# The first input product of the second layer, with x stationary over one token tile at a time, and four reorderings

## The chip, the cores and the metric

The kernel runs on one core of a Trainium2 chip. The metric is the device time of one execution in microseconds. An execution has an instruction stream for each engine: TensorE (PE in the profile, with its weight loads as PEld), VectorE (DVE), ScalarE (ACT), GpSimd (POOL) and SyncE (SP, which here only starts DMAs).

## The reference

A trunk of two layers works on one sequence of 256 tokens by 2048 features, all in float32. In outline:

```python
# layer 0
z, xbc, dt, q, k, v, gate = split(x @ in0_w)          # 2048 -> 13344 columns
ya = rms_norm(ssd(silu(conv(xbc)), softplus(dt)) * silu(z))
yb = causal_attention(rope(q), rope(k), v) * silu(gate)
x  = layer_norm(alpha * x + concat(ya, yb) @ out0_w)  # 4096 -> 2048
# layer 1
u, gate = split(x @ in1_w)                            # 2048 -> 2 * 2048
y  = gelu(s5(u))                                      # complex diagonal state space scan
ga, gb = split(y @ glu_w)                             # 2048 -> 2 * 2048
x  = layer_norm(alpha * x + (ga * sigmoid(gb) * silu(gate)) @ out1_w)
```

## The kernel before

**Units and their three products.** Every weight matrix is read as units of 512 KB: 256 input rows by 512 columns (`_chunk`), or 512 rows by 256 columns (`_half`). A unit is loaded into a `raw` tile by SP (L233), rounded into a high part `wh` by ACT (L236), and the rest `wl = raw - wh` is made by DVE (L238); `split_to(i)` does this for all units up to `i`. The pool has four buffers each for `raw`, `wh` and `wl`. The activations are kept as a high and a low part too. A product is the sum of high x high, high x low and low x high, on PE, in one of three forms:

- "x" (`xmm`, L282): the activations of one token tile (128 tokens) are the stationary operand, 512 weight columns move: 12 matmuls of 512 columns for a unit. The result has tokens on partitions.
- "w" (`wmm`, L303): 128 weight columns are stationary, 256 tokens move: 24 matmuls of 256 columns for a unit. The result has features on partitions.
- wide (`product_wide`, L336 and L337): weights stationary, the high and low activations move together as 512 columns, then 256 more: 8 pairs for a unit.

**The order of the work.** The instructions are written in program order and placed by a planner (`schedule_with_timeline_sim`), which simulates the engines and fills each engine's stream by priority and readiness. `tc.issue_after(i)` ties instructions to come behind `i` on `i`'s engine. Work other than the products waits in the list `jobs`; `pump` gives out some after each unit. A second list, `back`, is spread evenly over the units up to `goal[0]`; `finish` gives out what is left of it.

**The start.** `product_two` makes B and C together, the first unit of both first. Unit 0 is loaded and split in two pieces of 256 KB (L227 to L229), unit 1 whole. `dt_mm` and the five jobs of `dt_jobs` follow: two with a chain of polynomial steps on POOL (L516 to L527), then `soft4` (from L529), with L533 the DVE step that reads that chain's result, and `turn` (L547), which transposes what comes of it. They stand ahead of the four `cb_job`s.

**Constants of layer 1.** In layer 0's attention stage, `block_jobs(b)` prepares the scan's matrices for 16 blocks: `bars`, `efs`, `fcs` (DVE; `bars` also loads on SP), and for each pair `pes` (PE transposes and small matmuls, L761) and `mts` (six PE matmuls L771, ACT copies and two stores on ACT's queue).

**The seam.** The last output product of layer 0 is `product_apart`: ten units for both token tiles, then the last six (kept in a pool of their own) for tile 0, then the same six for tile 1. When tile 0 is done, `after0` adds the residual (`res0`: L1034, statistics L1035) and normalises (`norm_stats`, `scaled`: L1074 and L1077) while PE works on tile 1. `turned(t, f0, nf)` transposes `nf` blocks of 128 features on PE (`transpose4`, L412), rounds them on ACT (L1086) and makes the low part on DVE (L1090). Blocks 0 to 7 of tile 0 are turned by `mid`, ahead of the last unit of tile 1. Then PE runs 14 matmuls on a zero tile (`warm(WARM1)`, L421), turns two blocks of tile 1, and runs three more (`WARM2`). The first of layer 1's products follows in the form "w", which needs both token tiles of a block of features; the other blocks are normalised and turned by `prelude` between its units. The normalised activations lie in `x1t` with the 256 tokens in the order (token mod 4, token div 4).

**After the seam.** `first1` is the first quarter of u. `u_first` copies it to the tile `ut` (one buffer; L1152), `u_store` writes it to DRAM on POOL's queue (L1147), and the scan's steps (`steps`, two for each of 16 blocks, then `y_load` and `y_split`) go on `back`, with the goal ten units into the gated product. The other u quarters come in the wide form; `total` (L343, L344) adds their two halves. `y_split` (L1274, L1275) makes the high and low parts of y for the gated product, `product_pair`, whose units 6 and 7 are done last; `turn` in `glu_jobs` turns the gated result.

Of the kernel before, what the change touches and what calls it, by code (L numbers as in the profile page):

```python
# [9 lines left out]
F32 = mybir.dt.float32  # L10
F32R = mybir.dt.float32r
AF = mybir.ActivationFunctionType
# [4 lines left out]
P = 128  # L17
# [8 lines left out]
NKEEP = 6  # L26
WARM0 = 8
# [141 lines left out]
def trunk(tc, io, out):  # L169
# [8 lines left out]
    with ExitStack() as top:  # L178
# [34 lines left out]
        keep = [None, range(0)]  # L213

        def split_to(i):
            while nsplit[0] <= min(i, len(units) - 1):
# [5 lines left out]
                if n == 0:  # L222
                    wh = st.tile([P, UK, 512], F32R, tag="wh", name=nm("wh"))
                    wl = st.tile([P, UK, 512], F32R, tag="wl", name=nm("wl"))
                    for k in range(UK):
                        xpart(k)
# [11 lines left out]
                splits[n] = (loaded[-1], high, V.tensor_tensor(wl, raw, wh.bitcast(F32), op=OP.subtract))  # L238
# [38 lines left out]
        def xmm(ps, o, wpair, j, hk, start, stop):  # L277
            (xh, xl, xx), k = hk
            wh, wl = wpair
            sl = slice(o * P, o * P + P)  # L280
            for i, (l, r) in enumerate(((xh, wh), (xh, wl), (xl, wh))):
                T.matmul(ps[o], l[:, k, sl], r[:, j, :], start=start and i == 0, stop=stop and i == 2)  # L282
# [42 lines left out]
        def product_wide(hl, dst, then):  # L325
            for h in range(2):
# [14 lines left out]
                def total(o, ps=ps, h=h):  # L341
                    to = dst()[:, 2 * h + o, :]
                    A.activation(to, ps[o][:, 0:S], AF.Copy)  # L343
                    V.tensor_tensor(to, to, ps[o][:, S : 2 * S], op=OP.add)  # L344
# [22 lines left out]
        def product_two(hl, after):  # L367
            pss = [banks(), banks()]
            order = [(n, u) for u in range(PAIRED) for n in range(2)] + [(n, u) for n in range(2) for u in range(PAIRED, CU)]
            for at, (n, u) in enumerate(order):  # L370
                split_to(at + 3)
                parts = (((0, 1), (0, 1)), ((0, 1), (2,)))
                if at == 0:
# [7 lines left out]
        def product_apart(hl, nu, nk, after, mid=None):  # L381
            ps = banks()
            for u in range(nu - nk):
                split_to(unit[0] + 3 + u)
# [53 lines left out]
        with ExitStack() as l0:  # L438
# [139 lines left out]
            jobs.extend(dt_jobs())  # L578
# [117 lines left out]
            pend = []  # L696

            def block_jobs(b):
# [80 lines left out]
                return [bars, efs, fcs, pes, mts] if b % 2 else [bars, efs, fcs, lambda: pend.append(h)]  # L779
# [6 lines left out]
            def xs_jobs(ps, j):  # L786
# [13 lines left out]
                jobs.extend({0: [cb_job(g) for g in range(4)], 1: [trig_job], 2: [table_job]}.get(j, []))  # L800
# [255 lines left out]
        with ExitStack() as lt:  # L1056
# [22 lines left out]
            def turned(t, f0, nf):  # L1079
# [5 lines left out]
                hv, lv = (x1t[n][:, f0 : f0 + nf, :].rearrange("p f (s c) -> p f s c", s=4)[:, :, :, 32 * t : 32 * t + 32] for n in "hl")  # L1085
# [11 lines left out]
            def after0(ps, t):  # L1097
                def first():
# [4 lines left out]
                    scaled(t, 0, 2 if t else 4, norm_stats(st0, mr0, t))  # L1103

                jobs.append(first)
                jobs.extend([lambda: scaled(1, 2, 2)] if t else [lambda: scaled(0, 4, 4), lambda: scaled(0, 8, 4)])
# [8 lines left out]
            warm(WARM1)  # L1115
            end, tail["v"] = turned(1, 0, 2)
            with tc.issue_after(end.ins):
                warm(WARM2)
            x1 = x1n

            def rest0():
                tail["v"] = turned(1, 2, 2)[1]
# [4 lines left out]
            later = {1: [(1, 1)], 3: [(1, 2)], 5: [(0, 3), (1, 3)]}  # L1127
# [273 lines left out]
```

## Time and profile before

| | |
|---|---|
| median of 3 runs | 1340.22 us (1339.83 to 1340.71) |
| profiled execution, its own time | 1341.48 us |
| its span | 1339.7 us |
| PE busy | 1324.2 us (99%) |
| DVE, ACT, POOL busy | 960.9, 688.7, 336.6 us |
| granted PE clock, mean | 0.996 |
| DMA | 282.74 MB, 211 GB/s |

Times in the profile count from the span's start. L282 is line 282 of the kernel before. Matmuls are pipelined: one row's duration overlaps the next one's, so the rate is read from the starts, or from the chain of waits, where each piece counts only its own share. A busy PE says that instructions are in it, not that they are needed. The seam between the layers lies at about 849 to 886 us.

### The profile page before, as it was taken

The page shows a single profiled execution, that of the slowest core. Times are in us where ns is not written, and L with a number is a line of the kernel's source. Part 1 is how long each engine was busy: PE and PEld are TensorE (multiplying, and loading weights), DVE is VectorE, ACT ScalarE, POOL GpSimd, SP SyncE. Part 2 cuts the span into 40 slices and gives each one's busy share as a digit, 9 for nine tenths or more (in the row PEclk, how much of TensorE's full clock was granted, in tenths as well). Part 3 has the DMA queues.
Part 4 walks back from the last instruction along what each step waited for, and adds up shares of the span by engine and source line. Part 5 has one row for each costly group of instructions (what it writes and reads, how often), then busy time and mean ns, then how long its engine had stood idle before and what let it go on. Part 6 is the DMA issues. An engine that isn't in the chain of part 4 may idle for free.

```text
span 1339.7 us, 21680 instructions
## 1 busy us (share of the span) xinstructions
PE 1324.2 (99%) x8175; PEld 1119.6 (84%) x8175; DVE 960.9 (72%) x1604; ACT 688.7 (51%) x930; POOL 336.6 (25%) x648
## 2 busy tenths in 40 slices
PE   9999999999999999999999999999999999999996
PEld 8988888877888888888888888898888888888885
DVE  5677977876776876778788766749898845555556
ACT  5566668864644554554563444344345644444441
POOL 0042000121036148334887300013343100000001
PEclk9999999999999999999999999999999999999998
DMA  8555555444557557666757768397988675565662
GB/s 309 179 175 183 186 173 173 156 153 158 168 188 232 189 199 237 197 207 202 233 189 245 248 232 310 136 306 237 315 282 303 221 219 187 189 191 188 252 213 83
DMA packets 80729, 282.74 MB, mean 211 GB/s; under 512 B 9840, under 2 KB 12528, under 8 KB 80112
## 3 DMA queue, kind: packets, MB, share of 16 engines
q1 hardware_dynamic: 68112, 239.27, 53.9%
q0 software_dynamic: 7328, 30.42, 6.7%
q10 hardware_dynamic: 5184, 11.67, 2.4%
q8 instruction: 64, 1.05, 0.3%
q14 instruction: 41, 0.34, 0.1%
HBM read 260.34 MB, written 20.97 MB: 210 GB/s over the span
## 4 chain that ended last, share of the span: by engine, by line
PE 94%; POOL 2%; DVE 2%; DMA 1%; issue 1%; ACT 1%; SPq 0%; POOLq 0%; DVEq 0%; ACTq 0%
PE main L282 59%; PE main L336 14%; PE main L337 7%; PE main L303 5%; PE aux L412 2%; PE aux L850 1%; PE aux L761 1%; PE enc L1197 1%; PE dec L1242 1%; PE aux L939 1%; PE aux L971 1%; DVE wl L238 0%; DMA raw<-in_wi 0%; PE dec L1238 0%; POOL ew L527 0%
## 5 line engine op out<-in xcount | busy, mean ns | idle before, releaser
L238 DVE TENSOR_TENSOR wl<-raw,wh 128x1024 fp32r<-128x1024 f32 x431 | 533.0, 1238 | 321.8 <-ACT wh L236 317.6
L236 ACT ACTIVATE wh<-raw 128x1024 fp32r<-128x1024 f32 x431 | 455.7, 1059 | 530.9 <-PE main L282 328.4
L282 PE MATMUL main<-wh,A 128*128 128x512 f32 x1536 | 489.9, 394 | 0.0
L282 PEld LDWEIGHTS main<-wh,A 128*128 128x128 f32 x1536 | 287.8, 188 | 59.1 <-issue 0.3
L282 PE MATMUL main<-wl,A 128*128 128x512 f32 x768 | 300.8, 392 | 0.0
L336 PE MATMUL main<-A,wh 128*128 128x512 f32 x768 | 272.0, 398 | 0.0
L282 PE MATMUL main<-wh,C 128*128 128x512 f32 x768 | 241.4, 392 | 0.0
L337 PE MATMUL main<-A,wl 128*128 128x256 f32 x768 | 215.4, 281 | 0.0
L336 PEld LDWEIGHTS main<-A,wh 128*128 128x128 f32 x768 | 144.2, 188 | 33.9
L282 PEld LDWEIGHTS main<-wh,C 128*128 128x128 f32 x768 | 144.1, 188 | 30.6
L282 PEld LDWEIGHTS main<-wl,A 128*128 128x128 f32 x768 | 144.3, 188 | 29.2 <-issue 0.5
L282 PE MATMUL main<-wl,C 128*128 128x512 f32 x384 | 149.8, 390 | 0.0
L337 PEld LDWEIGHTS main<-A,wl 128*128 128x128 f32 x768 | 144.9, 189 | 0.2
L688 POOL TENSOR_TENSOR c<-c 128x8 f32<-128x8 f32 (+2 forms) x192 | 96.8, 522 | 25.8 <-DMA wb<-c 18.2
L282 PEld LDWEIGHTS main<-wl,C 128*128 128x128 f32 x384 | 72.1, 188 | 14.6
L336 PE MATMUL main<-C,wh 128*128 128x512 f32 x192 | 68.5, 400 | 0.0
L859 POOL TENSOR_TENSOR ssq<-ssq,c 128x256 f32<-128x256 f32 x16 | 18.4, 1147 | 171.6 <-ACT c L857 171.0
L912 POOL TENSOR_TENSOR b<-b 128x128 f32<-128x128 f32 x16 | 10.2, 639 | 194.6 <-DVE b L911 152.1
L337 PE MATMUL main<-C,wl 128*128 128x256 f32 x192 | 53.8, 281 | 0.0
L690 POOL TENSOR_TENSOR c<-c,c 128x4 f32<-128x4 f32 (+2 forms) x96 | 48.0, 500 | 7.4
L303 PE MATMUL main<-A,wh 128*128 128x256 f32 x256 | 44.1, 288 | 1.5 <-ACT wh L236 1.5
L691 POOL TENSOR_TENSOR c<-c,c 128x4 f32<-128x4 f32 (+2 forms) x96 | 45.5, 474 | 0.0
(287 smaller groups left out, 1451.4 us busy)
## 6 DMA issues: line engine op xcount, KB each, us to landing
raw<-in_wi SPq DMA_DIRECT2D x271, 512.0 KB, 3.5
raw<-in_wo SPq DMA_DIRECT2D x96, 512.0 KB, 4.3
raw<-in_wglu SPq DMA_DIRECT2D x64, 512.0 KB, 4.1
wt<-wb POOLq DMA_DIRECT2D x16, 896.0 KB, 8.1
wb<-ob ACTq DMA_DIRECT2D x16, 512.0 KB, 5.3
bc<-in_s5bc SPq DMA_DIRECT2D x16, 256.0 KB, 4.0
wb<-c POOLq DMA_DIRECT2D x16, 256.0 KB, 3.4
wb<-om ACTq DMA_DIRECT2D x16, 128.0 KB, 4.1
```

Source lines behind the costliest of these rows:

```text
L236: high = A.activation(wh, raw, AF.Copy)
L238: splits[n] = (loaded[-1], high, V.tensor_tensor(wl, raw, wh.bitcast(F32), op=OP.subtract))
L282: T.matmul(ps[o], l[:, k, sl], r[:, j, :], start=start and i == 0, stop=stop and i == 2)
L303: T.matmul(pv[o // 2][:, o % 2, :], l[:, j, sl], r[:, k, :], start=first and i == 0 and o % 2 == 0, stop=end and i == 2 and o % 2 == 1, sk ...
L336: T.matmul(ps[o], wh[:, j, sl], xx[:, k, :, :].rearrange("p a n -> p (a n)"), start=first, stop=False, skip_group_check=True)
L337: T.matmul(ps[o][:, S : 2 * S], wl[:, j, sl], xh[:, k, :], start=False, stop=end, skip_group_check=True)
L412: end = T.transpose(dst[:, i * P : i * P + P], s, ident)
L688: G.tensor_tensor(p[:, :, :, 0:m], cs[:, :, :, 1 : m + 1], cs[:, i, :, n : n + 1].unsqueeze(1).to_broadcast([P, 2, 4, m]), op=OP.mult)
L690: G.tensor_tensor(cs[:, 0, :, n + 1 : n + 1 + m], p0[:, 0, :, 0:m], p1[:, 1, :, 0:m], op=OP.subtract)
L691: G.tensor_tensor(cs[:, 1, :, n + 1 : n + 1 + m], p0[:, 1, :, 0:m], p1[:, 0, :, 0:m], op=OP.add)
L761: T.matmul(pk[at : at + 64, 64 * n + a * 16 : 64 * n + a * 16 + 16], d["ev"][:, a, 64 * i : 64 * i + 64], cv[:, a, i, :], start=True, stop ...
L859: G.tensor_tensor(ssq, ssq, jk[:, f, :], op=OP.add)
```

## The change

The first u product is written in the form "x". Its first four units (`NFIRST`) run over token tile 0, the first three of them directly behind the last output product, in place of the filler matmuls; tile 1 is normalised meanwhile on DVE, turned in four steps of four blocks, and the four units run again over tile 1. Units 4 to 7 run over both tiles. The order on DVE is tied from instruction to instruction, the low parts of the weights included (`hold`). The product now has tokens on partitions, so `u_first` copies it out, turns it back with eight transposes two units later, and only then stores it and puts the scan's steps on `back`. The tokens lie in `x1t` as (tile, token mod 4, rest), so that a tile is contiguous; `total`, `y_split` and the gated `turn` put the old order back, some of them in two pieces instead of one.

The four reorderings: unit 1 is loaded and split in two pieces as unit 0 is, and its matmuls are ordered by piece; `soft4` and `turn` of `dt_jobs` come behind the `cb_job`s, a column block later; `mts` of a pair comes behind `bars` of the next block; and `product_apart` prefetches no further than the first four units of the next product.

```diff
...
 NKEEP = 6
+NFIRST = 4
...
         keep = [None, range(0)]
+        hold = [None]
...
                 raw = st.tile([P, UK, 512], F32, tag="raw", name=nm("raw"))
-                if n == 0:
+                if n < 2:
...
                     for k in range(UK):
-                        xpart(k)
+                        if n == 0:
+                            xpart(k)
...
                 wl = pool.tile([P, UK, 512], F32R, tag=tl, name=nm("wl"))
-                splits[n] = (loaded[-1], high, V.tensor_tensor(wl, raw, wh.bitcast(F32), op=OP.subtract))
+                with ExitStack() as pin:
+                    if hold[0] is not None:
+                        pin.enter_context(tc.issue_after(hold[0]))
+                    splits[n] = (loaded[-1], high, V.tensor_tensor(wl, raw, wh.bitcast(F32), op=OP.subtract))
...
             for i, (l, r) in enumerate(((xh, wh), (xh, wl), (xl, wh))):
-                T.matmul(ps[o], l[:, k, sl], r[:, j, :], start=start and i == 0, stop=stop and i == 2)
+                end = T.matmul(ps[o], l[:, k, sl], r[:, j, :], start=start and i == 0, stop=stop and i == 2)
+            return end
...
-        def product_wide(hl, dst, then):
+        def product_wide(hl, dst, then, order=None):
...
                     to = dst()[:, 2 * h + o, :]
-                    A.activation(to, ps[o][:, 0:S], AF.Copy)
-                    V.tensor_tensor(to, to, ps[o][:, S : 2 * S], op=OP.add)
+                    one, two = ps[o][:, 0:S], ps[o][:, S : 2 * S]
+                    if order:
+                        to = to.rearrange("p (s t c) -> p t s c", s=4, t=2)
+                        one, two = (v.rearrange("p (t s c) -> p t s c", s=4, t=2) for v in (one, two))
+                    A.activation(to, one, AF.Copy)
+                    V.tensor_tensor(to, to, two, op=OP.add)
...
                 parts = (((0, 1), (0, 1)), ((0, 1), (2,)))
-                if at == 0:
+                if at < 2:
...
             ps = banks()
+            cap = unit[0] + nu + NFIRST - 1
             for u in range(nu - nk):
-                split_to(unit[0] + 3 + u)
+                split_to(min(unit[0] + 3 + u, cap))
...
             jobs.append(dt_mm)
-            jobs.extend(dt_jobs())
+            dtj = dt_jobs()
+            jobs.extend(dtj[:3])
...
             pend = []
+            late = []
...
-                return [bars, efs, fcs, pes, mts] if b % 2 else [bars, efs, fcs, lambda: pend.append(h)]
+                if b % 2:
+                    late.append(mts)
+                    return [bars, efs, fcs, pes] + ([mts] if b == 15 else [])
+                return [bars] + ([late[-1]] if late else []) + [efs, fcs, lambda: pend.append(h)]
...
                 held.extend([back(0), back(1)])
-                jobs.extend({0: [cb_job(g) for g in range(4)], 1: [trig_job], 2: [table_job]}.get(j, []))
+                jobs.extend({0: [cb_job(g) for g in range(4)] + dtj[3:], 1: [trig_job], 2: [table_job]}.get(j, []))
...
                 pv = px[:, 0 : nf * P].rearrange("p (f c s) -> p f s c", f=nf, s=4)
-                hv, lv = (x1t[n][:, f0 : f0 + nf, :].rearrange("p f (s c) -> p f s c", s=4)[:, :, :, 32 * t : 32 * t + 32] for n in "hl")
+                hv, lv = (x1t[n][:, f0 : f0 + nf, t * P : t * P + P].rearrange("p f (s c) -> p f s c", s=4) for n in "hl")
...
                         res0(tp.tile([P, 2, 512], F32, tag="xr", name=nm("xr")), ps, 3, (t,))
-                    scaled(t, 0, 2 if t else 4, norm_stats(st0, mr0, t))
+                    scaled(t, 0, 4, norm_stats(st0, mr0, t))
...
                 jobs.append(first)
-                jobs.extend([lambda: scaled(1, 2, 2)] if t else [lambda: scaled(0, 4, 4), lambda: scaled(0, 8, 4)])
+                jobs.extend([] if t else [lambda: scaled(0, 4, 4), lambda: scaled(0, 8, 4)])
...
             drain()
-            warm(WARM1)
-            end, tail["v"] = turned(1, 0, 2)
-            with tc.issue_after(end.ins):
-                warm(WARM2)
             x1 = x1n
-
-            def rest0():
-                tail["v"] = turned(1, 2, 2)[1]
...
-            later = {1: [(1, 1)], 3: [(1, 2)], 5: [(0, 3), (1, 3)]}
-            first1 = product("w", x1hl, prelude=lambda u: [turned(0, 8, 4) if u == 3 else None] + [step(t, i) for t, i in later.get(u, [])], first=(((0, 1), (0, 2)), rest0, ((0, 1), (1,))))
+            def first_product():
+                ps = banks()
+                base = unit[0]
+                split_to(base + NFIRST - 1)
+
+                end = {}
+
+                def mm(u, t):
+                    for j in range(UK):
+                        end["i"] = xmm(ps, t, ready[base + u], j, x1hl(u * UK + j), u == 0 and j == 0, u == CU - 1 and j == UK - 1)
+
+                def turn(t, f0):
+                    with tc.issue_after(end["i"].ins):
+                        end["t"], tail["v"] = turned(t, f0, 4)
+
+                def take(u):
+                    hold[0] = tail["v"].ins
+                    split_to(base + u)
+                    hold[0] = None
+                    tail["v"] = splits[base + u][2]
+
+                scaled(1, 4, 4)
+                for u in range(NFIRST - 1):
+                    mm(u, 0)
+                turn(1, 0)
+                with tc.issue_after(end["t"].ins):
+                    mm(NFIRST - 1, 0)
+                scaled(1, 8, 4)
+                turn(1, 4)
+                mm(0, 1)
+                take(4)
+                turn(0, 8)
+                mm(1, 1)
+                turn(1, 8)
+                take(5)
+                mm(2, 1)
+                scaled(0, 12, 4)
+                scaled(1, 12, 4)
+                mm(3, 1)
+                take(6)
+                turn(0, 12)
+                for u in range(NFIRST, CU):
+                    if u == 5:
+                        turn(1, 12)
+                        take(7)
+                    if u > 5:
+                        split_to(base + u + 2)
+                    for t in range(2):
+                        mm(u, t)
+                split_to(base + CU + 2)
+                for u in range(CU):
+                    ready.pop(base + u)
+                unit[0] += CU
+                return ps
+
+            first1 = first_product()
...
             def u_first(ps):
-                ut = u_tile()
-                for i in range(2):
-                    A.activation(ut[:, 2 * i : 2 * i + 2, :].rearrange("p f n -> p (f n)"), ps[i], AF.Copy)
-                u_store(ut, 0)
+                d = {}
+
+                def take():
+                    d["x"] = [w1("p1", [P, 2, 256]).rearrange("p a n -> p (a n)") for t in range(2)]
+                    for t in range(2):
+                        A.activation(d["x"][t], ps[t], AF.Copy)
+
+                def turn():
+                    ut = u_tile()
+                    px = sp.tile([P, 2, 512], F32, tag="enc", name=nm("turn"))
+                    for t in range(2):
+                        transpose4(px[:, t, :], [d["x"][t][:, f * P : f * P + P] for f in range(4)])
+                        A.activation(ut.rearrange("p f (s c) -> p f s c", s=4)[:, :, :, 32 * t : 32 * t + 32],
+                                     px[:, t, :].rearrange("p (f s c) -> p f s c", f=4, s=4), AF.Copy)
+                    u_store(ut, 0)
+                    back.extend([lambda fs=fs: [f() for f in fs] for t, fs in sorted(steps.items())])
+
+                return [take, lambda: None, turn]
...
                 fs = slice(4 * j, 4 * j + 4)
-                A.activation(y5["h"][:, fs, :], yt, AF.Copy)
-                V.tensor_tensor(y5["l"][:, fs, :], yt, y5["h"][:, fs, :].bitcast(F32), op=OP.subtract)
+                for t in range(2):
+                    yv = yt.rearrange("p f (s t c) -> p t f s c", s=4, t=2)[:, t]
+                    hv, lv = (y5[n][:, fs, t * P : t * P + P].rearrange("p f (s c) -> p f s c", s=4) for n in "hl")
+                    A.activation(hv, yv, AF.Copy)
+                    V.tensor_tensor(lv, yv, hv.bitcast(F32), op=OP.subtract)
...
-                    product_wide(x1hl, ut, lambda h, ut=ut, j=j: jobs.append(lambda: u_store(ut(), j)) if h else None)
+                    product_wide(x1hl, ut, lambda h, ut=ut, j=j: jobs.append(lambda: u_store(ut(), j)) if h else None, order=True)
...
                 if j == 0:
-                    jobs.append(lambda ps=ps: u_first(ps))
+                    jobs.extend(u_first(ps))
...
                 if j == 0:
-                    back.extend([lambda fs=fs: [f() for f in fs] for t, fs in sorted(steps.items())])
...
                     transpose4(px, [d["t"][:, o, f * P : f * P + P] for f in range(2) for o in range(2)])
-                    pv = px.rearrange("p (f s c) -> p f s c", f=2, s=4)
-                    ho, lo = (y[:, 2 * j : 2 * j + 2, :].rearrange("p f (c s) -> p f s c", s=4) for y in (y2h, y2l))
-                    A.activation(ho, pv, AF.Copy)
-                    V.tensor_tensor(lo, pv, ho.bitcast(F32), op=OP.subtract)
+                    for f in range(2):
+                        pv = px[:, f * S : f * S + S].rearrange("p (t s c) -> p t s c", t=2, s=4)
+                        ho, lo = (y[:, 2 * j + f, :].rearrange("p (t c s) -> p t s c", t=2, s=4) for y in (y2h, y2l))
+                        A.activation(ho, pv, AF.Copy)
+                        V.tensor_tensor(lo, pv, ho.bitcast(F32), op=OP.subtract)
...
                 jobs.extend([gate, rest, rest, turn])
...
```

## The prediction

> **What bounds the kernel now.** I read the page first, then what TensorE (PE) waited for, then the seam between the two layers in order of time, then the chain.
>
> ```profile
> span 1339.7 us, 21680 instructions
> PE 1324.2 (99%) x8175; PEld 1119.6 (84%) x8175; DVE 960.9 (72%) x1604; ACT 688.7 (51%) x930; POOL 336.6 (25%) x648
> ```
>
> What PE waited for in the whole span (total us, times, longest):
>
> ```profile
> PE main L303 <- ACT wh L236: 1.5, 1, 1.5
> PE main L303 <- DVE C L1090: 1.3, 1, 1.3
> PE aux L421 <- DVE idle L416: 1.0, 1, 1.0
> PE aux L547 <- DVE ew L533: 0.6, 1, 0.6
> ```
>
> PE is busy 99% and waits four times, 4.4 us in all. So nothing can be won by making another engine faster; the time can fall only where PE waits, or where its "busy" time is not needed work. The second kind is found at the seam. PE there, in order of time (start, us, line, count):
>
> ```profile
> 849.57 3.38 PE L421 MATMUL aux<-idle 128*128 128x512 f32 x14
> ...
> 859.71 1.82 PE L412 MATMUL aux<-consts,D 128*128 128x128 f32 x12
> 861.43 0.50 PE L303 MATMUL main<-C,wh 128*128 128x256 f32 x2
> 863.27 0.39 PE L303 MATMUL main<-C,wh 128*128 128x256 f32 x1 [1.34 <-DVE C L1090]
> ...
> 877.01 0.63 PE L336 MATMUL main<-C,wh 128*128 128x512 f32 x2
> ...
> 880.06 0.28 PE L303 MATMUL main<-C,wh 128*128 128x256 f32 x1
> ...
> 885.58 0.40 PE L336 MATMUL main<-C,wh 128*128 128x512 f32 x1
> ```
>
> Three stretches of the seam (us, busy time and count of PE, PEld, DVE, ACT, POOL, then granted clock, DMA share, GB/s):
>
> ```profile
> 849.57:853.70 4.13, 4.13 (x21) 3.17 (x19) 3.92 (x11) 0.59 (x2) 0.00 (x0) 1.00 0.00 0
> ...
> 859.71:863.27 3.56, 2.10 (x16) 1.51 (x14) 3.56 (x6) 2.52 (x4) 0.00 (x0) 1.00 0.47 147
> 863.27:866.69 3.42, 3.42 (x17) 3.42 (x18) 3.13 (x5) 0.00 (x0) 0.00 (x0) 0.54 0.46 158
> ```
>
> From 849.57 to 853.70 PE is fully "busy", but L421 is the filler on the idle tile: real work is two transposes. From 859.71 it turns twelve blocks, does two matmuls and waits for a low part (L1090); then for 3.42 us it works at a granted clock of 0.54. The seam costs time in three ways, and only one of them is a wait.
>
> **The first product.** The rates are in the chain (start, us, work):
>
> ```profile
> 847.48 0.87 PE aux L412 x8
> ...
> 880.23 5.51 PE main L303 x46
> ...
> 1065.06 8.38 PE main L282 x36
> ...
> 1074.30 35.81 PE main L282 x157
> ...
> 1118.96 21.81 PE main L282 x96
> ```
>
> A transpose is 0.87/8 = 0.109 us, a matmul with the weights stationary (L303) 5.51/46 = 0.120. The changed first product is the same 96 matmuls with x stationary as the last row: 8 units x 2 tiles x 6, 21.81 us unbroken. The old one is 192 x 0.120 = 23.0 us.
>
> Before: from 849.57 to 885.58 are 36.01 us. In the 3.05 us from 877.01 to 880.06 PE does eight pairs (L336 and L337), one whole unit of the next product, and only two matmuls of this one (0.24), so 2.81 us come off: 33.2 us.
> After: 21.81 + 24 transposes (8 blocks of tile 0, 16 of tile 1, as before) x 0.109 = 24.4 us, plus the turning back, 8 x 0.109 = 0.9: 25.3 us. The difference is 7.9 us, if PE never waits. Whether it does is decided on DVE, whose order the change pins from end to end:
>
> ```profile
> 848.59 1.29 DVE L1090 TENSOR_TENSOR C<-aux,C 128x512 fp32r<-128x512 f32 x2 [0.62 <-ACT C L1086]
> 849.79 0.68 DVE L1034 SCALAR_TENSOR_TENSOR D<-xr,main 128x512 f32<-128x512 f32 x1
> ...
> 851.60 0.47 DVE L1074 SCALAR_TENSOR_TENSOR D<-D,mr,row 128x256 f32<-128x256 f32 x1
> ...
> 857.61 0.75 DVE L1077 SCALAR_TENSOR_TENSOR D<-D,mr,row 128x512 f32<-128x512 f32 x1
> 858.27 0.75 DVE L1074 SCALAR_TENSOR_TENSOR D<-D,mr,row 128x512 f32<-128x512 f32 x1
> 858.94 1.22 DVE L238 TENSOR_TENSOR wl<-raw,wh 128x1024 fp32r<-128x1024 f32 x1
> 860.07 0.74 DVE L1077 SCALAR_TENSOR_TENSOR D<-D,mr,row 128x512 f32<-128x512 f32 x1
> ...
> 862.53 0.68 DVE L1090 TENSOR_TENSOR C<-aux,C 128x512 fp32r<-128x512 f32 x1
> ```
>
> A normalised piece of 512 (L1074 and L1077) is 1.3 to 1.5 us, a low part of x 0.6 to 0.7, a low part of a weight unit 1.13 to 1.22. Blocks 0 to 7 of tile 0 are finished about 849.9, so units 0 to 3 can run over tile 0 from 849.57, the first three until 853.7. DVE begins tile 1 at 849.79, as before; residual and statistics done, its first piece starts at 851.60 and, at 512 wide and with the reciprocal between, ends about 853.2, just ahead of the first transposes (853.7). I then laid PE's order (six matmuls 1.36, four transposes 0.44) against DVE's chain. The low part of blocks 0 to 3 ends about 855.6, wanted 856.3; low weights of unit 4 at 859.7 and x blocks 8 to 11 at 860.3 and 861.6, wanted 862.2 and 863.6; unit 5 at 862.7, wanted 865; blocks 12 to 15 at 867.4 and 868.0, wanted 868.5; unit 7 at 869.2, wanted 871.2. Every margin is between 0.5 and 2 us: no wait, but little cover. I allow 0.3 us for handovers; the bounds are 0, and 3.5 us if the thin ones all go. Raw weights are not the limit: their four buffers come free with the low parts of units 0 to 3, before the seam, and the prefetch beyond them that the cap removes could not be split anyway, as the split buffers are full.
>
> The clock: 3.42 x 0.46 = 1.6 us of the 7.9 are the stretch at 0.54, which followed 3.56 us of transposes and waiting. [...]
>
> **The turning back** also moves work. The store of the first u block leaves two units (2 x 2.81 = 5.6 us) later, and the scan's steps start with it. POOL's queue carries that store, the loads and the scan's tables behind it. The steps are spread anew over the units left to the same last unit, so the lag is made up on the way; what ends the scan is this:
>
> ```profile
> 1093.05 1.23 DVE L1275 TENSOR_TENSOR A<-ut,A 128x1024 fp32r<-128x1024 f32 x1 [2.58 <-ACT A L1274]
> ```
>
> ```profile
> 1061.32 0.39 PE L282 MATMUL main<-wh,A 128*128 128x512 f32 x1
> ```
>
> The last y is split at 1094.3. The product that needs it starts at 1061.32; 48 of its matmuls come before 1074.30 (a unit of 12, and the 36 at 1065.06), and the 145th reads that y: 1074.30 + 96 x 0.227 = 1096.1. Only 1.8 us of cover. Halving the split (one piece per token tile) adds two fixed costs but lets DVE start sooner; I take 0, with up to 3 us if the last steps fall a unit behind. The single u tile is a further wait: the second u block must wait on ACT until the store has landed, with weight splits queued behind it. The splits run three units ahead of PE (some 8 us), so it costs nothing unless the store takes over twice this:
>
> ```profile
> ud<-ut POOLq DMA_DIRECT2D x2, 512.0 KB, 3.8
> ```
>
> **The start.** PE and ACT at the second unit:
>
> ```profile
> 8.16 0.64 PE L303 MATMUL main<-A,wl 128*128 128x256 f32 x4
> 10.25 2.18 PE L303 MATMUL main<-A,wh 128*128 128x256 f32 x16 [1.46 <-ACT wh L236]
> ```
>
> ```profile
> 6.42 0.63 ACT L228 ACTIVATE wh<-raw 128x512 fp32r<-128x512 f32 x1 [1.43 <-DMA raw<-in_wi]
> 9.14 1.06 ACT L236 ACTIVATE wh<-raw 128x1024 fp32r<-128x1024 f32 x1 [2.09 <-DMA raw<-in_wi]
> 10.11 0.61 ACT L456 ACTIVATE A<-a 128x512 fp32r<-128x512 f32 x1
> 11.09 1.06 ACT L236 ACTIVATE wh<-raw 128x1024 fp32r<-128x1024 f32 x1 [0.37 <-DMA raw<-in_wi]
> ```
>
> In halves, the first half of unit 1 lands about midway between 6.42 and 9.14, say 7.8, and is rounded by 8.4, before PE is done at 8.64. So the 1.6 us gap closes. But unit 2 is rounded at 12.15 whatever is done (ACT waits for its DMA), and PE would want it at 8.64 + 24 x 0.120 = 11.5; it took it at 8.64 + 1.61 + 2.9 = 13.1. Gain 1.0 us, bounds 0 and 1.6. On SP's queue the extra DMA puts the next loads one issue later.
>
> **The other three edits.** The later softplus end (`dtj[3:]`) takes away PE's 0.6 us for L533, which ends POOL's long chain: gain 0.6, bounds 0 and 0.7, as the scan needs it far later. `mts` behind the next block's `bars` moves six matmuls, ACT copies and two stores on ACT's queue past `bars`' load on SP and its DVE work; the list of PE's waits has none there, so 0 from both sides. The permuted layout and split copies in `total`, `y_split` and `turn` cost ACT some 0.2 us a time (2 x 0.63 against 1.06 above) and DVE as little, hidden under PE: 0.
>
> **The sum** for the profiled execution (span 1339.7, its own time 1341.48): 7.9 - 0.3 + 1.0 + 0.6 = 9.2 us less, 1332.3. The median of the runs shown is 1.26 lower than that execution, so 1331.0.
>
> **The rivals.** (1) PE waits at the seam: the planner puts the turning of tile 0's last four blocks ahead of unit 4. These want the normalised piece at 864.2, PE is there at 862.2: 2 us, and what follows inherits up to 1.5 more. For it: the before trace has just such a misplaced turning at 859.71. Against: unit 4 is ready first. 1333 to 1334.5, chance 0.20. [...] Chance 0.06. (3) The change doesn't do what it says: the planner starts no x matmuls at 849.57, and the filler's 3.9 us stay as a wait: 1335. Against: their operands are ready and nothing else is. Chance 0.08. (4) Slower: the scan's tail. Beyond its 1.8 us of cover each us of delay is a us of PE wait; to end over 0.2% slower than before it must lose 9.2 + 2.7 + 1.8 = 13.7 us, five units at the end of the list, then 1343 or more. Against: the same last unit. Chance 0.04.
>
> **How the numbers follow.** The forecast has 0.62; 1331.0 is its own. The upper end 1335.5 takes in rivals 1 and 3; the lower end 1328.8 takes the start at 1.6, no handovers, and a unit's worth (some 1.5 us) for small waits that the records hide. About 0.2% (2.7 us) is what a measurement can tell from no change: all but rival 4 and a mixture of losses to about 1338 clear it. Faster 0.92, same 0.04, slower 0.04.
>
> **What would show it.** Right: no L421 after the first microseconds; x-stationary matmuls directly behind the last output product; clock 1.00 through the seam; the first product ended some 8 to 9 us earlier relative to 849.57; PE's wait list without L533 and with under 0.8 us at unit 2. Wrong: a PE wait on L1090, L1074 or L238 over 1 us in the seam, a second half-clock stretch, or a wait on L1275 at the gated product.

## The result, and the profile after

The changed kernel takes 1338.04 us (median of 22 runs, 1336.15 to 1342.72), the kernel before 1339.97 us in 22 runs beside them (1338.28 to 1343.95). The ratio is 0.9986, with a 95% interval of 0.998 to 0.9992: 1.9 us faster, between 1.1 and 2.7. The forecast was 9.2 us, and its range ended at 1335.5.

The profiled execution after has a time of its own of 1336.96 us. The page:

```profile
span 1335.2 us, 21514 instructions
PE 1318.7 (99%) x8070; PEld 1110.2 (83%) x8070; DVE 960.1 (72%) x1614; ACT 692.6 (52%) x946; POOL 343.4 (26%) x648
```

The two profiled executions are 4.5 us apart, the medians 1.9. The one before lay 1.5 above its median, the one after 1.1 below. So terms read from the two traces add up to more than was won.

What PE waited for after the change (us in total, times, longest):

```profile
PE aux L559 <- DVE ew L545: 2.1, 1, 2.1
PE main L310 <- ACT wh L231: 1.2, 3, 0.5
PE aux L433 <- DVE idle L428: 1.0, 1, 1.0
PE main L343 <- DVE ut L355: 0.7, 1, 0.7
PE main L288 <- ACT C L1103: 0.3, 1, 0.3
```

L545 is L533 of before, L231 and L310 are L228 and L303, L433 is L421, L424 is L412, L343 and L344 are L336 and L337, L288 is L282, L355 is L344, L539 is L527, L559 is L547, L1103 is L1086. The wait on L1090 is gone. The wait on the step behind POOL's chain, which was to go, has grown from 0.6 to 2.1. The wait for the u tile is new.

PE through the seam after the change, in order of time (start, us, line, count):

```profile
848.56 1.03 PE L424 MATMUL aux<-consts,D 128*128 128x128 f32 x8
...
850.81 0.39 PE L288 MATMUL main<-wh,C 128*128 128x512 f32 x1
...
854.90 0.60 PE L424 MATMUL aux<-consts,D 128*128 128x128 f32 x4
...
857.18 0.60 PE L424 MATMUL aux<-consts,D 128*128 128x128 f32 x4
...
858.57 0.60 PE L424 MATMUL aux<-consts,D 128*128 128x128 f32 x4
...
860.86 0.60 PE L424 MATMUL aux<-consts,D 128*128 128x128 f32 x4
...
869.06 1.03 PE L424 MATMUL aux<-consts,D 128*128 128x128 f32 x8
869.85 0.71 PE L343 MATMUL main<-C,wh 128*128 128x512 f32 x2
870.90 0.50 PE L288 MATMUL main<-wh,C 128*128 128x512 f32 x1 [0.34 <-ACT C L1103]
...
876.50 0.40 PE L344 MATMUL main<-C,wl 128*128 128x256 f32 x2
```

The first product reads C from 850.81, directly behind the output product, with no filler between. The next product takes over at 876.50. From these 25.69 us come off the two matmuls of the next product at 869.85 (2 x 0.227), so it takes 25.2 us, one wait of 0.34 included. The same work took 33.2 us before: at the seam 8.0 us were won.

Three stretches after the change (us, busy time of PE, PEld, DVE, ACT, POOL, granted clock, DMA share, GB/s):

```profile
107.20:110.60 3.40, 1.30 (x8) 0.90 (x7) 1.25 (x4) 0.00 (x0) 1.91 (x3) 1.00 0.00 0
110.60:114.00 3.40, 3.40 (x13) 2.61 (x12) 3.34 (x7) 2.06 (x5) 0.00 (x0) 0.50 0.27 60
...
848.50:872.00 23.50, 23.16 (x118) 18.92 (x117) 17.42 (x26) 10.80 (x15) 2.89 (x8) 1.00 0.25 86
```

The clock is full through the seam. The half-clock stretch now stands at 110.6, behind the wait on L545.

To see where time went, the two profiles were laid side by side at equal numbers of columns of the big products done. A unit is 6144 columns, and there are 432. The changed kernel is 0.9 us ahead after the start. Between the 20th and the 30th unit it falls back by 2.6, since the `cb_job`s now come there, and by another 1.5 at the step behind POOL's chain. At the 60th unit, when the same work is done in both, it is 1.1 behind: 2.0 us have been lost. It wins 8.1 at the seam, and gives 2.3 back in the 110 us behind it.

### The profile page after: what moved, and what is told of

The parts are those of the page before. It is cut to its first block, busy times and chain, and to the rows that moved or that the text cites. A ratio compares the mean times of both kernels' runs of the same rounds, so it can differ in the third digit from the quotient of the medians.

```text
span 1335.2 us, 21514 instructions
## 1 busy us (share of the span) xinstructions
PE 1318.7 (99%) x8070; PEld 1110.2 (83%) x8070; DVE 960.1 (72%) x1614; ACT 692.6 (52%) x946; POOL 343.4 (26%) x648
## 4 chain that ended last, share of the span: by engine, by line
PE 95%; POOL 2%; DMA 2%; DVE 1%; ACT 0%; issue 0%; SPq 0%; POOLq 0%; ACTq 0%; DVEq 0%
PE main L288 60%; PE main L343 15%; PE main L344 8%; PE main L310 3%; PE aux L424 2%; DMA raw<-in_wi 1%; PE aux L867 1%; PE aux L775 1%; PE enc L1275 1%; PE dec L1320 1%; PE aux L956 1%; PE aux L988 1%; POOL ew L528 0%; PE dec L1316 0%; DMA ud<-ut 0%; PE aux L785 0%
## 5 line engine op out<-in xcount | busy, mean ns | idle before, releaser
L288 PE MATMUL main<-wh,A 128*128 128x512 f32 x1536 | 489.9, 394 | 0.0
L288 PEld LDWEIGHTS main<-wh,A 128*128 128x128 f32 x1536 | 287.8, 188 | 59.1 <-issue 0.3
L288 PE MATMUL main<-wl,A 128*128 128x512 f32 x768 | 300.7, 392 | 0.0
L343 PE MATMUL main<-A,wh 128*128 128x512 f32 x768 | 272.9, 399 | 0.0
L288 PE MATMUL main<-wh,C 128*128 128x512 f32 x832 | 262.0, 392 | 0.3 <-ACT C L1103 0.3
L344 PE MATMUL main<-A,wl 128*128 128x256 f32 x768 | 215.3, 280 | 0.0
L288 PEld LDWEIGHTS main<-wh,C 128*128 128x128 f32 x832 | 155.6, 188 | 33.5 <-ACT C L1103 1.0
L343 PEld LDWEIGHTS main<-A,wh 128*128 128x128 f32 x768 | 144.8, 188 | 33.5
L288 PEld LDWEIGHTS main<-wl,A 128*128 128x128 f32 x768 | 144.3, 188 | 29.3 <-issue 0.5
L288 PE MATMUL main<-wl,C 128*128 128x512 f32 x416 | 162.3, 390 | 0.0
L344 PEld LDWEIGHTS main<-A,wl 128*128 128x128 f32 x768 | 145.3, 189 | 0.3
L701 POOL TENSOR_TENSOR c<-c 128x8 f32<-128x8 f32 (+2 forms) x192 | 99.8, 538 | 23.6 <-DMA wb<-c 16.0
L288 PEld LDWEIGHTS main<-wl,C 128*128 128x128 f32 x416 | 78.1, 188 | 16.1
L343 PE MATMUL main<-C,wh 128*128 128x512 f32 x192 | 68.4, 400 | 0.7 <-DVE ut L355 0.7
L344 PE MATMUL main<-C,wl 128*128 128x256 f32 x192 | 53.3, 282 | 0.0
L310 PE MATMUL main<-A,wh 128*128 128x256 f32 x256 | 43.5, 284 | 1.2 <-ACT wh L231 1.2
```

The costliest lines, as they stand in the source:

```text
L288: end = T.matmul(ps[o], l[:, k, sl], r[:, j, :], start=start and i == 0, stop=stop and i == 2)
L310: T.matmul(pv[o // 2][:, o % 2, :], l[:, j, sl], r[:, k, :], start=first and i == 0 and o % 2 == 0, stop=end and i == 2 and o % 2 == 1, sk ...
L343: T.matmul(ps[o], wh[:, j, sl], xx[:, k, :, :].rearrange("p a n -> p (a n)"), start=first, stop=False, skip_group_check=True)
L344: T.matmul(ps[o][:, S : 2 * S], wl[:, j, sl], xh[:, k, :], start=False, stop=end, skip_group_check=True)
L701: G.tensor_tensor(p[:, :, :, 0:m], cs[:, :, :, 1 : m + 1], cs[:, i, :, n : n + 1].unsqueeze(1).to_broadcast([P, 2, 4, m]), op=OP.mult)
```

## The experiments

**The softplus end alone.** The kernel before with the `dt_jobs` edit and nothing else:

```diff
-            jobs.extend(dt_jobs())
+            dtj = dt_jobs()
+            jobs.extend(dtj[:3])
...
-                jobs.extend({0: [cb_job(g) for g in range(4)], 1: [trig_job], 2: [table_job]}.get(j, []))
+                jobs.extend({0: [cb_job(g) for g in range(4)] + dtj[3:], 1: [trig_job], 2: [table_job]}.get(j, []))
```

> The kernel before with the later softplus end alone. Theory A: PE's wait grows from 0.6 to 2 us, with a half-clock stretch behind it: 1.5 to 3 us slower than before. Theory B: wait about 0.6 to 1.0 us, time within 0.6 us of before. The prediction had 0.6 us faster.

Measured: 1343.93 us, ratio 1.0024 (1.0015 to 1.0034) to 1340.66: 3.2 us slower by itself. Its waits of PE, then the stretch behind them:

```profile
PE aux L547 <- DVE ew L533: 2.3, 1, 2.3
```

```profile
110.97:114.38 3.41, 3.41 (x13) 2.62 (x13) 3.34 (x7) 2.06 (x5) 0.00 (x0) 0.50 0.11 20
```

The wait is 1.8 longer than before's 0.56, and 3.41 us at a granted clock of 0.50 follow, which would be some 1.7 more (an estimate, half of 3.41). The sum of 3.5 is near the 3.2 measured, but the trace doesn't bear it out term by term. From the 20th to the 60th unit PE takes 126.6 us here, 124.4 in before, and 123.7 in before_again and before_third (the same kernel, see below): 2.2 to 2.9 us are lost. Some of the sum is won back behind the stretch; how isn't followed up.

Why the wait grew is seen where POOL's chain begins (L516) and at the step that waits for its end, first in before, then in only_dt:

```profile
84.46 1.63 POOL L516 TENSOR_TENSOR ew<-dw 32x256 f32<-32x256 f32 x1 [82.91 <-ACT a L563]
...
109.40 0.24 PE L547 MATMUL aux<-consts,ew 32*128 32x32 f32 x1 [0.56 <-DVE ew L533]
```

```profile
83.98 6.61 POOL L516 TENSOR_TENSOR ew<-dw 32x256 f32<-32x256 f32 x1 [82.43 <-ACT a L563]
...
110.57 0.24 PE L547 MATMUL aux<-consts,ew 32*128 32x32 f32 x1 [2.34 <-DVE ew L533]
```

Taking its wait off, PE is ready for the step at 108.84 in before and at 108.23 in only_dt, 0.6 us sooner. POOL's chain takes 24.4 us in before and 26.1 in only_dt (its first row alone 6.61 instead of 1.63) and ends 1.2 us later. Together these are the 1.8. The edit moved other work too: with `soft4` behind them, the four `cb_job`s run on DVE and PE while POOL's chain is under way. Why POOL's rows are longer then isn't shown.

**The same step put back, and put later still.** The changed kernel with the `dt_jobs` order of before (dt_early), and with the step one column block later (dt_late):

```diff
-                jobs.extend({0: [cb_job(g) for g in range(4)] + dtj[3:], 1: [trig_job], 2: [table_job]}.get(j, []))
+                jobs.extend({0: [cb_job(g) for g in range(4)], 1: dtj[3:] + [trig_job], 2: [table_job]}.get(j, []))
```

> The changed kernel with the softplus end and its transposes (soft4, turn) back ahead of the cb jobs. Theory A: the reordering itself put the transposes ahead of the end of POOL's chain in PE's stream. Then PE's wait falls from 2.1 to about 0.6 us, the half-clock stretch at 110 us goes, and the time is 2.5 to 3.5 us under the changed kernel (some 1335). Theory B: POOL's chain ends at about 109 us whatever the order, and the 0.93 us won at the start merely arrive there earlier. Then a wait of 1.5 us or more stays, and the time is within 1 us of the changed kernel.

> The changed kernel with soft4 and turn one more column block later. Both theories: POOL's chain has ended by then, PE does not wait, no half-clock stretch at 110 us, 2.5 to 4 us under the changed kernel (1334 to 1335.5). If neither holds, the planner puts the transposes at the same place again and the time is that of the changed kernel.

Measured: dt_early 1336.29 us, ratio 0.997 (0.9958 to 0.9982); dt_late 1334.34, ratio 0.9961 (0.9946 to 0.9975). Both are below the changed kernel. By the ratios dt_early is 4.0 us below before, dt_late 5.2 and the changed kernel 1.9. So putting the step back is worth 2.1, putting it later 3.3; the edit alone cost 3.2. In dt_early the wait on this step is back at 0.6, and a wait of 1.7 us stands on a step of the scan (L1315) where no other profile has more than 0.4. How the step stands to POOL's chain, first in the changed kernel, then in dt_late:

```profile
108.57 0.71 POOL L539 TENSOR_TENSOR ew<-ew 32x256 f32<-32x256 f32 x1
109.31 0.41 DVE L545 SCALAR_TENSOR_TENSOR ew<-ew,dw 32x256 f32<-32x256 f32 x1 [5.00 <-POOL ew L539]
109.78 0.24 PE L559 MATMUL aux<-consts,ew 32*128 32x32 f32 x1 [2.10 <-DVE ew L545]
```

```profile
111.36 0.73 POOL L539 TENSOR_TENSOR ew<-ew 32x256 f32<-32x256 f32 x1
118.76 0.40 DVE L545 SCALAR_TENSOR_TENSOR ew<-ew,dw 32x256 f32<-32x256 f32 x1
122.66 0.24 PE L559 MATMUL aux<-consts,ew 32*128 32x32 f32 x1
```

In dt_late the chain ends at 112.1 and PE comes ten microseconds later, without a wait. In the changed kernel PE stands in front of it, as before. Counted in columns of the big products, PE has done 34.2 units when it comes to the first of these transposes in before and in dt_early, 33.2 in only_dt and in the changed kernel, and 38.4 in dt_late. So the job that was moved behind the `cb_job`s came one unit (2.8 us) sooner on PE in the order of the work. In time it came only 0.6 us sooner (only_dt against before), since the `cb_job`s' matmuls (some 2.4 us) now stand ahead of it. Why the planner placed it so isn't shown.

**The start alone.** The kernel before with unit 1 in two pieces (`n < 2`, `at < 2`):

> The kernel before with unit 1 loaded and split in two pieces alone. Theory A: 0.9 us faster, as PE's wait at POOL's chain stays at 0.6. Theory B: the wait there grows to about 1.5 us and takes the gain back: within 0.3 us of before.

Measured: 1339.11, ratio 0.9992 (0.9984 to 1.0001): 1.1 us, though the interval just reaches no change. The traces bear a gain out: PE has done ten units at 35.5 to 36.3 us in the eight profiles with the old start, and at 34.9 to 35.7 in the six with the new one, 0.8 apart in the mean. At POOL's chain PE doesn't wait here at all, which neither theory had.

**`mts` alone.**

```diff
-                return [bars, efs, fcs, pes, mts] if b % 2 else [bars, efs, fcs, lambda: pend.append(h)]
+                if b % 2:
+                    late.append(mts)
+                    return [bars, efs, fcs, pes] + ([mts] if b == 15 else [])
+                return [bars] + ([late[-1]] if late else []) + [efs, fcs, lambda: pend.append(h)]
```

> The kernel before with the later mts alone. The prediction had 0 from both sides: within 0.7 us of before, PE's list of waits unchanged between 110 and 850 us. Rival: some of the spread of the changed kernel's time comes from here, 0.8 us or more either way.

Measured: 1340.26, ratio 0.9999 (0.999 to 1.0008): nothing, as forecast.

**The seam alone.** The kernel before with the first product, the turning back, the permuted layout and the cap, without the other three edits:

> The kernel before with the x-stationary first product, its turning back, the layout and the prefetch cap, and none of the other three reorderings. Theory S: the seam is 6.4 us shorter where the kernel before has no half-clock stretch there and 8.1 where it has one, and the turning back gives some 2.4 back (8 transposes 0.9, ACT's and PE's wait for the u tile 0.9, the rest small): 3 to 5 us faster. Rival: the seam's gain exists only beside the half-clock stretch of the one profiled execution, and ordinary runs are within 1.5 us of before.

Measured: 1335.48, ratio 0.9966 (0.9953 to 0.9978) to 1339.98: 4.5 us, where 7.6 were forecast for this part. Its product runs from 848.64 to 874.31, 25.67 us, as in the changed kernel, so the missing 3 us are not in the product.

**The kernel before, profiled twice more.** Of what the seam was to win, 1.6 us were the stretch at half clock.

> The kernel before, profiled again, for the stretch at half clock at the seam. In the profiles so far with the old seam it stood in two of four (before at 863.3, only_dt at 865.3; not in only_start and only_mts), behind the same wait of 1.3 us. Theory A (it comes in some executions and not in others): about one profile in two of this same kernel lacks it, with a span 1.5 to 1.7 us shorter than 1339.7. Theory B (the kernel's own order decides): it is there in every profile of the kernel before, from about 863 to 866.7, at a granted clock of about 0.54.

> The same kernel and question once more. Theory A (in some executions): one of the two profiles, more or less, lacks the half-clock stretch at the seam. Theory B (the kernel's order decides): both have it, from about 863 to 866.7 at a granted clock of about 0.54.

They have spans of 1337.8 and 1337.2 us, against 1339.7 in the first profile, and neither has the stretch. In before_third, the wait of PE, and then the seam as a whole and the 3.41 us behind the wait:

```profile
PE main L303 <- DVE C L1090: 1.3, 1, 1.3
```

```profile
848.52:883.02 34.50, 33.02 (x250) 31.10 (x249) 22.88 (x33) 12.47 (x17) 3.76 (x8) 1.00 0.55 201
862.31:865.72 3.41, 3.41 (x29) 3.41 (x30) 3.04 (x5) 0.64 (x1) 0.00 (x0) 1.00 0.50 159
```

The same wait of 1.3, but the clock stays at 1.00 and the seam takes 34.50 us instead of 36.01. Of the six profiles with the old seam and this wait (before three times, only_dt, only_start, only_mts), two have the stretch. Without it the seam wins 34.50 - 2.81 - 25.2 = 6.5 us and not 8.0; with the 2.3 given back behind it that is 4.2, close to the 4.5 of the seam alone.

The wait on L533 that the softplus edit was to take away is no fixture either: before has 0.6, before_again and before_third have none, as POOL's chain took 23.1 and 23.0 us there and not 24.4.

**The filler taken out.** The kernel before with `WARM1 = 1` and `WARM2 = 1`, which asks what the filler itself was worth:

> The kernel before with the filler at the seam cut from 14 and 3 matmuls to 1 and 1, which do no needed work. [...]

Measured: 1339.9, ratio 0.9998 (0.999 to 1.0007). PE's wait, and the clock behind it:

```profile
PE aux L412 <- DVE D L1077: 2.8, 1, 2.8
```

```profile
851.90:855.40 3.50, 3.23 (x14) 2.86 (x15) 2.60 (x6) 0.77 (x2) 0.00 (x0) 0.53 0.00 0
862.00:866.00 4.00, 4.00 (x36) 3.95 (x35) 3.04 (x5) 2.25 (x4) 3.27 (x8) 1.00 0.86 262
```

Here the clock halves behind the open gap (0.53 over 851.90 to 855.40), and not later (1.00 over 862.00 to 866.00); the time is the same. With the filler in its place the clock was 1.00 over 849.57 to 853.70 and on to 859.71 in before. That the filler held the clock there fits these two profiles; that it saved time is not borne out. Even with the stretch at half clock this seam is 1.0 us further on than in before_again when the first product is done. PE then waits for the scan's load, and the lead is gone:

```profile
PE enc L1197 <- DMA um<-ud: 1.2, 1, 1.2
```

In this trace, then, a seam that is 1 us shorter is given back at the scan, without any turning back.

**What is given back behind the seam.** The store of the first u block and what waited for it, in the changed kernel (ACT, POOL and PE in order of time), and then the store's group among the DMA issues (count, KB each, median us to landing):

```profile
892.29 0.58 ACT L1226 ACTIVATE ut<-turn 128x512 f32<-128x512 f32 x1
893.16 0.78 POOL L1211 DMA_DIRECT2D ud<-ut  x1 [22.68 <-ACT ut L1226]
...
899.14 0.94 ACT L354 ACTIVATE ut<-main 128x256 f32<-128x256 f32 x3 [1.55 <-DMA ud<-ut]
899.34 0.71 POOL L1241 DMA_DIRECT2D um<-ud  x1 [5.40 <-DMA ud<-ut]
...
900.13 0.47 PE L343 MATMUL main<-C,wh 128*128 128x512 f32 x1 [0.74 <-DVE ut L355]
```

```profile
ud<-ut POOLq DMA_DIRECT2D x4, 512.0 KB, 6.2
```

The store is issued at 893.16 and has landed at 899.1, 6 us later. Until then ACT can't copy the second u block into the one `ut` buffer, and PE waits 0.74 us for its accumulators. Set side by side, the intervals between matmuls behind the seam hold 0.7 us for the eight transposes, 0.9 at that wait, and 0.8 spread over the scan's first loads and steps: together about the 2.3 us. Two versions of dt_late were run. The first gives the first block tiles of its own (ut_own). The second also turns it back a unit sooner and gives out the scan's steps a unit behind that (scan_gap):

```diff
-                    ut = u_tile()
+                    uh = [w1("p2", [P, 2, 256]) for _ in range(2)]
...
-                    u_store(ut, 0)
+                    dst = ud[0].rearrange("g a c -> (g a c)").rearrange("(f p t) -> p f t", p=P, t=S)
+                    for h in range(2):
...
+                        nc.gpsimd.dma_start(dst[:, 2 * h : 2 * h + 2, :], uh[h])
```

```diff
-                    back.extend([lambda fs=fs: [f() for f in fs] for t, fs in sorted(steps.items())])
-
-                return [take, lambda: None, turn]
+                return [take, turn, lambda: back.extend([lambda fs=fs: [f() for f in fs] for t, fs in sorted(steps.items())])]
```

> The dt_late kernel with the first u block written to two tiles of its own (p2) and stored in two halves, so that the second u block need not wait for its store. Theory U: ACT's wait at the u tile for the store (1.5 us in the changed kernel) and PE's wait of 0.7 behind it go: 0.7 to 1.0 us less than dt_late. Rival: the scan's later start is what costs, and a wait at its first loads takes the place: no change, or a new wait on um.

> The version with its own tiles for the first u block (ut_own, 7.0 us below the kernel before), with the turn one unit sooner and the scan's steps given out from one unit later, so that the store has landed when they load it. Theory A (the 1.5 us that PE waits there for the load is a cost by itself): that wait goes and the time is 1 to 1.5 us below ut_own, some 8 to 8.5 us below the kernel before, 1331.5 to 1332 where that is 1340. Theory B (the store's own time sets it, or another wait comes in its place): no change against ut_own, about 7 us below, 1333.

Measured: ut_own 1332.98, ratio 0.9948 (0.9936 to 0.9961); scan_gap 1333.93, ratio 0.995 (0.9939 to 0.9962) to 1340.52. Both beat the kernel before by 6.6 to 7.0 us and the changed kernel by some 5, of which 3.3 are dt_late's; neither is told apart from dt_late. ut_own's longest wait of PE, then scan_gap's first and last:

```profile
PE enc L1278 <- DMA um<-ud: 1.5, 1, 1.5
```

```profile
PE main L310 <- ACT wh L231: 1.2, 2, 0.9
...
PE enc L1276 <- DMA um<-ud: 0.2, 1, 0.2
```

The wait for the tile went and a wait for the scan's load came; that went too, and the time did not move. These waits are not a price that can be taken off one by one.

At last, only_seam without the turning back, which leaves the first u block in the wrong order:

```diff
-                return [take, lambda: None, turn]
+                ut = u_tile()
+                for i in range(2):
+                    A.activation(ut[:, 2 * i : 2 * i + 2, :].rearrange("p f n -> p (f n)"), ps[i], AF.Copy)
+                u_store(ut, 0)
```

> The first product alone is changed (as in only_seam, which came out 4.5 us below the kernel before), but its result is not turned back: it is copied out and stored as it lies, as in the kernel before, so the first u block is left in the wrong order and the later results are not the reference's; the work of every other step is the same. Theory A (turning back costs what the matmul intervals after the seam add up to, about 2.4 us: eight transposes 0.9, the wait of about 0.9 for the u tile, and what follows from the later store): about 6.9 us below the kernel before, 1333 where that is 1340, and no wait of PE on DVE's ut. Theory B (turning back costs its eight transposes alone, 0.9): about 5.4 us below, 1334.6. Theory C (the 2 us given back after the seam come from the split copies of the permuted order, not from turning back): as only_seam, about 4.5 us below, 1335.5.

Measured: 1337.47 (1334.07 to 1338.78), ratio 0.997 (0.9958 to 0.9982): not faster than only_seam. Its longest wait of PE, and the stretch around it:

```profile
PE enc L1256 <- issue: 1.7, 1, 1.7
```

```profile
913.20:916.60 3.40, 3.40 (x40) 2.89 (x40) 3.40 (x8) 0.00 (x0) 0.17 (x2) 0.53 0.99 377
```

The transposes and the wait for the tile are gone. The scan's first step on PE comes at 897.0 instead of 902.8. But PE stands idle for 1.7 us ahead of a later step of the scan (the trace names no one that it waits for), and in this profile a half-clock stretch follows (0.53 over the row above). So this run doesn't price the turning back; neither theory that gave it a gain came true. The time agrees with theory C, but what that blames, the split copies, isn't shown: the wait that took the place is on the scan.

## Why the prediction was wrong, point by point

The sign was right, and so was the mechanism at the seam. Two terms of the sum were wrong and a third was too small. Of the 7.3 us by which the forecast was too high, the parts run alone put 3.8 on the softplus end and 3.1 on the seam with what lies behind it.

**"gain 0.6, bounds 0 and 0.7", the softplus end: wrong in sign.** Measured by itself it is a loss of 3.2 us. The step that failed is "takes away PE's 0.6 us for L533": later in the list of jobs was read as later on PE, and POOL's chain was taken to end when it had. On PE the step came one unit sooner in the order and 0.6 us sooner in time, POOL's chain ended 1.2 later, and the wait grew from 0.6 to 2.3 (only_dt). The bounds excluded a loss with a reason (the scan needs the result far later) that concerned the reader of the result and not the engine that waits for its input. The prediction did not ask what the `cb_job`s, now ahead of the step, do to PE's order and to POOL. The half clock behind the wait (0.50 over 3.41 us in only_dt) was not foreseen either. And the 0.6 itself stands in one of the three profiles of the kernel before, so there was little to win in most executions.

**"33.2 ... 25.3, the difference is 7.9 us": right in this profile, too large for the median.** The new seam took 25.2 us, and its order is that which was laid out: x matmuls from the end of the output product, transposes by four at 854.90, 857.18, 858.57 and 860.86, every margin held but that of blocks 12 to 15 (0.34 us, about the 0.3 allowed for handovers). But the 1.6 us at half clock belonged to the profiled execution; two further profiles of the same kernel lack them. The sum counted them as a gain, and then took the gain off a median that lies 1.26 us below the profiled execution and so, probably, mostly lacks them. That counts much the same microseconds twice. That the stretch "followed 3.56 us of transposes and waiting" holds for that one execution: in before_third the same transposes and the same wait left the clock at 1.00 (862.31 to 865.72).

**"plus the turning back, 8 x 0.109 = 0.9": about 2.3 went behind the seam.** The transposes themselves are 0.7. The sentence on the single u tile gave the condition itself, "unless the store takes over twice this" (3.8 us): the store took 6 us, not twice, and PE waited all the same (0.74 us), since ACT's copy frees PE's accumulators and was needed at once. No single run here isolates this term: leaving it out brought another wait, and no_filler gave back 1 us at the scan with no turning back at all. So how much of the 2.3 is the turning back stays open.

**The start, 1.0; `mts`, 0; the permuted layout.** The start measured 1.1, `mts` 0. The size of the start came out, its reason didn't. The prediction had PE wait for unit 2 and so stop at 1.0 of 1.6. In the changed profile PE doesn't wait at unit 2 (it comes there at 12.31, and the unit is rounded by 11.84). The 1.2 us in the list are three waits at the halves of the first two units (0.19, 0.44, 0.54), which had been given none. The scan's tail, which had 1.8 us of cover, shows no wait. The terms given for the range's lower end add up to 1328.6 and not 1328.8; nothing hangs on that.

Taken singly the parts measured -4.5 (seam), +3.2 (softplus end), -1.1 (start) and 0: together -2.4 us, inside the interval of the -1.9 measured for the whole (-2.7 to -1.1). The forecast had -7.6, -0.6, -1.0 and 0.

**The rivals.** None came true: PE did not wait 2 us at the seam, the clock was 1.00 there (848.50 to 872.00; the chance of 0.06 was for half clock at the seam), the x matmuls started where they should, and no tail was lost. The change gave its gain back at a place for which there was no rival at all, a smaller edit that had been given one sentence.

## What to carry to other kernels

Where a planner places the instructions, a job that is moved in the list has to be followed to its place on the engine, and so have the jobs that it lets pass: here an edit for 0.6 us cost 3.2, as PE came a little sooner and what it waited for came later. A stretch at half clock, or a wait of half a microsecond, in one profile is a property of that execution until a second profile shows it again, and it shouldn't be counted both in a stage and in the distance to the median. A small edit bundled with a large one is best run alone first: with this one put back the change is worth about twice as much (4.0 us against 1.9), and with the step put later still 5.2.

## What the runs showed of the hardware

**When the granted clock changed.** In the profiles of before and after, the changes of the granted clock lie whole multiples of 3.413 us apart, counted from the first rise. In before the rise is at 6.81 (the matmuls of 256 columns are 0.23 us apart from 4.74 and 0.12 from 7.17), the half-clock stretch from 863.56 to 866.97, and the last fall at 1331.18, which are 251, 252 and 388 steps. In after the rise is at 4.80, the stretch from 110.61 to 114.03, and the last fall at 1329.17: 31, 32 and 388 steps. The first rise differs between these two executions by 2.0 us, so the same wait lies elsewhere between the steps. At the seam the stretch stands in two of six profiles with the same wait of 1.3 us; whether that comes of it isn't shown. What decides in a given stretch of 3.41 us isn't settled: PE was busy 1.95 us of the one before the half clock in before (860.15 to 863.56), and 1.93 of that in before_third (858.90 to 862.31), after which the clock stayed at 1.00.

**Half clock behind waits of 2 to 3 us.** Waits of 2.1 (the changed kernel), 2.3 (only_dt) and 2.8 us (no_filler) were each followed by a half-clock stretch: 0.50 over 3.41 us in the first two, 0.53 over 851.90 to 855.40 in no_filler. Waits of 1.7 us came out both ways: a stretch followed in no_turn (0.53 over 913.20 to 916.60), and none in dt_early (1.00 over 986.06 to 989.47, where the wait lies; the mean of the whole execution is 0.997, against 0.996 in no_turn). In this kernel a wait of two microseconds has to be priced at up to 1.7 more (an estimate, half of the 3.41 at 0.50); at the seam the traces with and without the stretch differ by 1.5 (36.01 and 34.50).
